# Layer 1's triangular inverses, taken pair by pair from k's projection on, in small steps between dense products

## The chip, the core and the metric

The kernel runs on one NeuronCore of one Trainium2 chip. The core has TensorE (PE in the profile; its weight loads are PEld), VectorE (DVE), ScalarE (ACT), GpSimd (POOL) and SyncE (SP), which here issues every transfer. Each takes its instructions in order and waits on semaphores. The metric is the device time of one execution in microseconds, as the median of several runs; lower is better.

## The reference, cut to what matters

One inference step through two layers, 1104 token columns in all (64 of samples, 16 meta tokens, 1024 of a prompt). Layer 0 is a gated DeltaNet and is not touched. Layer 1 is RWKV-7 time mixing:

```python
xs = xn[None] + xx[None] * mu[:, None, None, :]          # six token-shifted inputs
rkvz = jnp.einsum('sbtd,sde->sbte', xs[:4], w_rkvz)       # r, k, v, z: 1024 x 1024 each
w = -jax.nn.softplus(-(w0 + jnp.tanh(xs[4] @ w1) @ w2)) - 0.5
a = jax.nn.sigmoid(a0 + (xs[5] @ a1) @ a2)
kk = l2norm((k * k_k).reshape(B, T, H, N))
k = k * (1.0 + (a - 1.0) * k_a)
decay = jnp.exp(-jnp.exp(w))
b_h = kk * a_h
def step(S, inp):                                         # once per token
    r_t, k_t, v_t, d_t, kk_t, b_t = inp
    S = (S * d_t[:, :, None, :]
         + jnp.einsum('bhvk,bhk->bhv', S, -kk_t)[..., None] * b_t[:, :, None, :]
         + v_t[..., None] * k_t[:, :, None, :])
    return S, jnp.einsum('bhvk,bhk->bhv', S, r_t)
```

16 heads of width 64. The kernel takes the scan in chunks of 64 tokens: within a chunk each token's update depends on the earlier ones through a 64 x 64 unit lower triangle, made of products of the keys (kk, decayed) with kk * a, and the chunk needs that triangle's inverse. The triangles depend on k, on the decay w and on the rate a, but not on r, v or z.

## The kernel before

**Layout.** Channels lie on partitions and tokens along the free axis, in three segments of 384, 384 and 336 columns (SEGS, padded to 1152 in DRAM). A *pair* is one of 8 groups of 128 channels, two heads; an *item* is one pair in one segment: 6 chunks x 2 heads. There are 24 items. Dense products are taken in three terms (high and low parts of input and weight), so that one tile of 128 outputs by 1024 inputs costs 72 matmuls (24 for each segment). PSUM tiles carry a letter of their tag in front of their names in the profile: d for dense products, f for short-lived ones, m for the merges.

**Order.** Nothing is placed by hand. The program is written down in one order; a planner then fills each engine's queue: at each planned moment an engine takes, of what it could run by then (inputs there, a buffer free), the instruction that was written first. What is written early runs early if it can, and gives way otherwise. On the chip the queues are then fixed and in order. Buffers go around by tag: a tag with two buffers lets a third user wait. A pool that takes the place of closed ones gets its first tile when what overlaps it is through.

**The stages around the change.** At the end of layer 0, `gdn_out_norm` normalises the activations, with a pool "rnorm" on the right end of SBUF, directly under the xb tiles; `lora_first` (L1107) makes the hidden rows hh and hl of the two low-rank projections, and mixes k's inputs into slots. Then `layer1` (L1681):

1. `keys_decay_rate` (L1155), with a pool "lora": zero pads for five DRAM arrays, the second low-rank weights (w2: the matrices of w and of a), and then for each pair p: the 72 products of k's tile (`project`, L1145, stores it to kd), `lora_second` (L1135) for w with a sigmoid and a running sum (csd), and for a with a sigmoid (ad). Weights come by `load_w` (L189) through the tags wraw (2 buffers), whi and wlo (3 each).
2. A pool "rinv" for the inverses opens when "lora" is closed. A loop of 16 tiles, eight of r and then eight of v; before each eight, `mix` (L1011) makes eight inputs in eight of eleven slots, taken around in turn (a slot is two rows of xa or xc, or two tiles of xn2). After the tiles 1, 3, 5, 7 and 9 one call of `rwkv_inverse` (L1279) writes down a batch of five items, the last of four.
3. `rwkv_inverse`: for each item it loads csd, ad and kd (one item ahead), makes the keys (`rwkv_keys`, L1256: kk with a scale, Dp and iD with Exp; `alpha`, L1267, for al), 12 products of al with kk for the triangles (tile fL, stored to rltd) and one for the keys' row sums (frss, stored to rssd). Then, for the batch: `block_scale` (L487), and `inverse_blocks` (L455), which reloads the triangles' 32 x 32 diagonal blocks as rows, inverts them all at once on VectorE by 31 steps of two instructions (`inverse32`, L440), sends the result through DRAM into T1n and TT; and for each item `inverse_merge` (L504): 12 products (mY), a scaling on VectorE (invY), 12 more (mU), a copy, and a store to ttd.
4. `mix_out` stores two segments of z's input; `rwkv_gates` (L1027) makes z's first segment, 8 tiles of 24 products (tile dz), with its inputs in xa.
5. The pools close, and the recurrence begins: `rwkv_front` (L1323) reloads everything for an item, `rwkv_step` runs the chunks. Items there are numbered by segment and then pair, n = 8 s + p.

## Time and profile before

| what | us |
|---|---|
| median of 3 runs | 2517.23 (2510.52 to 2519.47) |
| the profiled execution | 2503.36 |
| its span, first to last instruction | 2501.6 |
| k's projection, from the last product of `lora_first` on | about 1396 to 1508 |
| r's eight tiles | about 1508 to 1640 |
| v's eight tiles | about 1640 to 1802 |
| z's first segment | about 1802 to 1866 |

In the views a time is in microseconds from the span's start. A row of a timeline gives start, length, engine, line, operation, out<-in, shapes, a count of instructions merged into the row, and in brackets how long the engine had been idle and what ended that. A row of a stretch gives for each engine its busy time and its number of instructions, then the granted clock of TensorE, the share of the DMA engines and GB/s. A row of waits gives who waited for whom: total us, times, longest. A row of groups gives count, busy time, mean length in ns, idle time before and what ended it. Matmuls are pipelined: a matmul of 384 columns has 0.34 us in a row, but the next one starts about 0.17 us after it, so PE's busy time tells whether it had work, and counts of matmuls tell how much it got done.

### The profile page before, as it was taken

How to read it: one execution, taken by the hardware profiler on the slowest of the kernel's cores; microseconds unless marked ns; L12 is line 12 of the kernel's file. 1: busy time of each engine (PE TensorE's matmuls, PEld its weight loads, DVE VectorE, ACT ScalarE, POOL GpSimd, SP SyncE). 2: the span in 40 equal slices, each digit the busy share in tenths (PEclk: the TensorE clock that was granted, in tenths of full speed). 3: DMA queues.
4: the chain of work that ended last, by engine and by line, in shares of the span. 5: the costliest groups of instructions: out<-in, count | busy, mean ns of one | idle time of the engine just before them, and what ended most of it. 6: DMA issues, size and time to landing. Idle time of an engine off the chain costs nothing. (4 is left out here: it accounts for less than half of the span.)

```text
span 2501.6 us, 52567 instructions
## 1 busy us (share of the span) xinstructions
PE 2305.2 (92%) x18593; PEld 2065.5 (83%) x18593; DVE 1698.5 (68%) x4268; ACT 1423.3 (57%) x3913; POOL 1148.4 (46%) x1404
## 2 busy tenths in 40 slices
PE   6998999999898989999989999988879999999996
PEld 5887988888797889789989998877768777877875
DVE  7779686876849585863357535697875678667563
ACT  5456555564646565565344557464444567678663
POOL 4554444444444354432214425453347565656653
PEclk9999999999999999999999999999988999999997
DMA  3323333333232333353251445767565444343331
GB/s 107 100 72 98 83 106 83 95 85 85 79 91 77 87 89 85 92 147 118 89 147 60 117 167 180 170 184 202 145 181 170 126 133 121 94 140 88 110 97 50
DMA packets 471939, 284.65 MB, mean 114 GB/s; under 512 B 187482, under 2 KB 457051, under 8 KB 471675
## 3 DMA queue, kind: packets, MB, share of 16 engines
q1 hardware_dynamic: 471674, 281.29, 40.0%
q8 instruction: 147, 2.41, 0.4%
q14 instruction: 118, 0.96, 0.1%
HBM read 200.00 MB, written 81.17 MB: 112 GB/s over the span
## 5 line engine op out<-in xcount | busy, mean ns | idle before, releaser
L86 POOL TENSOR_TENSOR wlo<-wraw,whi 128x512 fp32r<-128x512 f32 x260 | 347.8, 1340 | 350.9 <-ACT whi L82 311.9
L82 ACT CAST whi<-wraw 128x512 fp32r<-128x512 f32 x260 | 160.1, 617 | 168.7 <-PE dq L76 43.6
L76 PE MATMUL d<-xc,whi 128*128 128x384 f32 (+3 forms) x846 | 238.2, 339 | 0.3 <-ACT ev L1152 0.3
L450 DVE TENSOR_TENSOR invtmp<-invA,invT 72x31 f32<-72x31 f32 (+31 forms) x403 | 184.7, 458 | 20.8 <-DMA invA<-ltd 7.6
L452 DVE TENSOR_TENSOR invT<-invT,invtmp 72x31 f32<-72x31 f32 (+31 forms) x403 | 187.6, 466 | 6.9
L76 PEld LDWEIGHTS d<-xc,whi 128*128 128x128 f32 (+1 forms) x846 | 155.0, 190 | 7.3 <-issue 4.6
L76 PE MATMUL dz<-xc,whi 128*128 128x384 f32 (+1 forms) x480 | 149.6, 343 | 0.0
L76 PE MATMUL dv<-xc,whi 128*128 128x384 f32 (+1 forms) x480 | 149.4, 343 | 0.0
L417 DVE SCALAR_TENSOR_TENSOR cvy<-raw,cw,cvy 128x408 f32<-128x408 f32 (+2 forms) x192 | 128.9, 674 | 28.7 <-POOL cvy L415 27.4
L76 PE MATMUL dz<-xa,whi 128*128 128x384 f32 (+1 forms) x416 | 139.4, 357 | 4.8 <-ACT whi L82 2.4
L76 PE MATMUL d<-xa,whi 128*128 128x384 f32 (+3 forms) x450 | 140.0, 344 | 3.9 <-ACT xa L82 2.5
L415 POOL TENSOR_TENSOR cvy<-cvy,cvz 128x408 f32<-128x408 f32 (+2 forms) x96 | 99.7, 1039 | 70.5 <-ACT cvz L62 51.3
L76 PE MATMUL d<-xc,wlo 128*128 128x384 f32 (+2 forms) x396 | 130.5, 339 | 0.0
L76 PE MATMUL rA<-rS,AR 128*64 128x128 f32 x512 | 106.0, 289 | 8.7 <-DVE rS L1439 5.0
L76 PE MATMUL rA<-UV,G 128*64 128x64 f32 x1152 | 112.4, 223 | 0.4 <-ACT UV L62 0.4
L76 PE MATMUL dv<-xa,whi 128*128 128x384 f32 (+1 forms) x288 | 101.4, 352 | 8.9 <-ACT raw L401 6.9
L76 PEld LDWEIGHTS rA<-UV,G 128*64 128x64 f32 x1152 | 101.7, 138 | 3.3 <-issue 1.4
L62 ACT ACTIVATE o<-rA,gcol 128x128 f32<-128x128 f32 x128 | 46.2, 367 | 90.0 <-DVE S L774 89.6
L62 ACT ACTIVATE raw<-cvy 128x408 f32<-128x408 f32 (+2 forms) x96 | 49.5, 516 | 82.1 <-DVE cvy L417 80.6
L1439 DVE SCALAR_TENSOR_TENSOR rS<-rA,DC,pre 64x64 f32<-64x64 f32 x256 | 72.2, 282 | 31.6 <-PE rA L76 26.6
L62 ACT ACTIVATE rX<-rA,rk 64x64 f32<-64x64 f32 x272 | 83.7, 308 | 16.9 <-PE rA L76 10.9
L76 PE MATMUL dz<-xa,wlo 128*128 128x384 f32 (+1 forms) x256 | 90.5, 354 | 2.9 <-POOL wlo L86 2.9
(510 smaller groups left out, 7730.1 us busy)
## 6 DMA issues: line engine op xcount, KB each, us to landing
wraw<-in_gdn_w_in SPq DMA_DIRECT2D x96, 256.0 KB
wraw<-in_rwkv_w_rkvz SPq DMA_DIRECT2D x96, 256.0 KB
Sb<-in_state_gdn SPq DMA_DIRECT2D x64, 256.0 KB
wraw<-in_rwkv_w_o SPq DMA_DIRECT2D x48, 256.0 KB
E<-drow SPq DMA_DIRECT2D x24, 384.0 KB
attn<-drow SPq DMA_DIRECT2D x24, 384.0 KB
wraw<-in_gdn_w_out SPq DMA_DIRECT2D x36, 256.0 KB
out_s_gdn<-Sb SPq DMA_DIRECT2D x32, 256.0 KB
```

The costliest lines, as they stand in the source:

```text
L62: return self.nc.scalar.activation(out, in_, func, bias=bias, scale=scale, **kw)
L76: self.nc.tensor.matmul(out, lhsT, rhs, start=start, stop=stop)
L82: nc.scalar.copy(hi, x)
L86: e.tensor_tensor(lo, x, hi.bitcast(F32), op=ALU.subtract)
L415: nc.gpsimd.tensor_tensor(y[:, 0:wd], y[:, 0:wd], y1[:, 0:wd], op=ALU.add)
L417: nc.vector.scalar_tensor_tensor(y[:, 0:wd], raw[:, k:k + wd], cw[k], y[:, 0:wd], op0=ALU.mult, op1=ALU.add)
L450: nc.vector.tensor_tensor(tmp, A[:, j, j + 1:32].unsqueeze(2).broadcast_to([nb, n, m]), Tv[:, j, 0:m].unsqueeze(1).broadcast_to([nb, n, m] ...
L452: nc.vector.tensor_tensor(Tv[:, j + 1:32, 0:m], Tv[:, j + 1:32, 0:m], tmp, op=ALU.subtract)
L1439: nc.vector.scalar_tensor_tensor(S[hs[h], h, :], dS, DC[hs[h], ci:ci + 1], pre[hs[h], hs[h]], op0=ALU.mult, op1=ALU.add)
```

## The change

The inverses are started in k's projection. Items are numbered n = 3 p + s, so that a pair's three items follow one another, and the first can be made when the pair's k, w and a are there. `rwkv_inverse` becomes a generator that stops between small steps (48 in all): the keys of an item are made one step before its triangles' products, a batch's blocks are a step, and its merges come two to a step. At each stop it tells which pair must be projected before it goes on. After each of k's tiles two steps are taken, after each of r's and v's tiles three, and at the end what is left.

To have "rinv" open beside "lora", memory is rearranged: "lora" moves to the right end of SBUF; the raw w2 loses its tile and comes in four pieces through wraw, written down ahead of k's first weights; the zero pads shrink to one row that is broadcast; the loaded keys and the tiles T1n and L21 lie in xa; invA has one buffer, and Y and the row sums share a tile. Since xa's first four rows are taken by that, the mixed inputs go around in nine slots instead of eleven. The row-scale column and ttd's place follow the new numbering.

```diff
@@ inverse_blocks, inverse_merge
-        A = self.t(pool, [128, 1024], "invA", 2)[0:nb]
+        A = self.t(pool, [128, 1024], "invA", 1)[0:nb]
...
-        Y = self.t(pool, [128, 192], "invY", 2)[:, 0:32 * n].rearrange("p (c i) -> p c i", i=32)
+        Y = self.inv_yk[:, 192 * (th0 // 6 % 2):192 * (th0 // 6 % 2) + 32 * n].rearrange("p (c i) -> p c i", i=32)
@@ mix
-        xs = [self.slots[(self.slot + k) % 11] for k in range(8)]
+        xs = [self.slots[2 + (self.slot + k) % 9] for k in range(8)]
@@ keys_decay_rate
-        with self.tc.tile_pool(name="lora", bufs=1, reuse_waits="tile") as pool:
-            z = t(pool, [128, 8, 48], "zpad")
+        with self.tc.tile_pool(name="lora", bufs=1, side="right", reuse_waits="tile") as pool:
+            z = t(pool, [128, 48], "zpad")
...
-                nc.sync.dma_start(d[:, :, NT:1152].rearrange("k p n -> p k n"), z)
+                nc.sync.dma_start(d[:, :, NT:1152].rearrange("k p n -> p k n"), z.unsqueeze(1).broadcast_to([128, 8, 48]))
...
-            wr = t(pool, [128, 2, D], "lw2")
-            for q in (0, 64):
-                nc.sync.dma_start(wr[q:q + 64, 0], i["rwkv_w2"][0])
-                nc.sync.dma_start(wr[q:q + 64, 1], i["rwkv_a2"][0])
             w2 = t(pool, [128, 2, D], "lw2h", dt=F32R), t(pool, [128, 2, D], "lw2l", dt=F32R)
-            nc.scalar.copy(w2[0], wr)
-
-            for u, q in ((0, slice(0, 64)), (1, slice(64, 128))):
-                nc.vector.tensor_tensor(w2[1][q, u], wr[q, u], w2[0][q, u].bitcast(F32), op=ALU.subtract)
+            for u, (nm, q) in enumerate((("rwkv_w2", slice(0, 64)), ("rwkv_a2", slice(64, 128)))):
                 nc.gpsimd.memset(w2[1][64 - q.start:128 - q.start, u].bitcast(F32), 0.0)
+                for c in (0, 512):
+                    wr = t(self.wp, [128, 4, 128], "wraw", 2).rearrange("p k m -> p (k m)")
+                    for a in (0, 64):
+                        nc.sync.dma_start(wr[a:a + 64], i[nm][0][:, c:c + 512])
+                    nc.scalar.copy(w2[0][:, u, c:c + 512], wr)
+                    nc.vector.tensor_tensor(w2[1][q, u, c:c + 512], wr[q], w2[0][q, u, c:c + 512].bitcast(F32), op=ALU.subtract)
...
                 self.lora_second(1, k, hl, w2, dst_a)
+                self.inverse_go(2, k)
@@ the steps
+    def inverse_go(self, n, done):
+        while n and self.inv_need is not None and self.inv_need <= done:
+            self.inv_need = next(self.inv, None)
+            n -= 1
+
+    def inverse_load(self, n):
+        p, s = divmod(n, 3)
+        c0 = SEGS[s][0]
+        ld = dict(zip(("cs", "a", "k"), self.inv_ld[n % 2]))
+        for nm, d in (("cs", self.csd), ("a", self.ad), ("k", self.kd)):
+            self.nc.sync.dma_start(ld[nm], d[p][:, c0:c0 + 384])
+        return ld
+
+    def inverse_keys(self, n, pool):
+        nc, t = self.nc, self.t
+        p, s = divmod(n, 3)
+        ld = self.inverse_load(n)
+        kk, Dp, iD = self.rwkv_keys(p, ld, pool, "s")
+        sq = t(pool, [128, 384], "sgl", 2)
+        self.act(sq, kk, AF.Square)
+        al = t(pool, [128, 6, 64], "sal", 1)
+        self.alpha(al, kk, Dp, s, nc.vector)
+        nc.gpsimd.tensor_tensor(kk, kk, ld["a"], op=ALU.mult)
+        nc.vector.tensor_tensor(kk, kk, iD, op=ALU.mult)
+        return kk, al, sq
@@ rwkv_inverse
+        nxt = self.inverse_keys(items[0], pool)
         for q, n in enumerate(items):
-            s, p = divmod(n, 8)
...
-            ld = self.ahead or self.rwkv_load(n, pool, "s", names)
-            kk, Dp, iD = self.rwkv_keys(p, ld, pool, "s")
-
-            self.ahead = self.rwkv_load(n + 1, pool, "s", names) if n < 23 else None
...
+            yield min(n + 1, items[-1]) // 3
+            kk, al, sq = nxt
+            if n < items[-1]:
+                nxt = self.inverse_keys(n + 1, pool)
             gp = self.ps("f", 2, "L")
...
+        yield 0
         rk2 = self.rk2[:, 30 * b:30 * b + nth]
         blk = self.block_scale(ssd, rk2, pool)
         TT = [t(pool, [128, 6, 64], "sTT", 3) for _ in items]
-        T1n, L21 = t(pool, [128, 30, 32], "T1n", 1), t(pool, [128, 30, 32], "L21", 1)
+        T1n, L21 = self.inv_bl
         self.inverse_blocks(f"r{b}", ltd, blk, pool, TT, T1n[:, 0:nth], L21[:, 0:nth], nth)
         for q, n in enumerate(items):
+            if q % 2 == 0:
+                yield 0
             self.inverse_merge(L21, TT[q], T1n, rk2[:, 6 * q:6 * q + 6], pool, 6 * q, 6)
-            nc.sync.dma_start(self.ttd[n], TT[q].rearrange("p c k -> p (c k)"))
+            nc.sync.dma_start(self.ttd[8 * (n % 3) + n // 3], TT[q].rearrange("p c k -> p (c k)"))
+        yield min(items[-1] + 1, 23) // 3
@@ layer1
-        self.keys_decay_rate(x, self.hh, self.hl)
         ip = pool("rinv", ctx)
         self.rwkv_masks(ip, True)
+        self.inv_yk = self.t(ip, [128, 384], "invYK")
+        flat = xa.rearrange("p k n -> p (k n)").bitcast(F32)
+        self.inv_ld = [[flat[:, 384 * (3 * u + v):384 * (3 * u + v) + 384] for v in range(3)] for u in (0, 1)]
+        self.inv_bl = [flat[:, 2304 + 960 * u:3264 + 960 * u].rearrange("p (c i) -> p c i", i=32) for u in (0, 1)]
+        self.inv, self.inv_need = (p for b in range(5) for p in self.rwkv_inverse(b, ip)), 0
+        self.keys_decay_rate(x, self.hh, self.hl)
...
-            if n in (1, 3, 5, 7, 9):
-                self.rwkv_inverse((1, 3, 5, 7, 9).index(n), ip)
+            self.inverse_go(3, 7)
         self.mix_out(3, xb)
+        self.inverse_go(99, 7)
```

More of the change, by code (lines that the diff above doesn't have):

```diff
@@ L1275, in alpha @@
                                   kk[:, 0:64].rearrange("p (b r) -> p b r", r=8)[:, :, 0:1])
-    ahead = None
+    def inverse_go(self, n, done):
[21 more added lines that the diff above has]
+        return kk, al, sq
     def rwkv_inverse(self, b, pool):
@@ L1284, in rwkv_inverse @@
         ltd, ssd = self.dram([nth, 128, 64], f"rltd{b}"), self.dram([nth, 128], f"rssd{b}")
+        nxt = self.inverse_keys(items[0], pool)
         for q, n in enumerate(items):
-            s, p = divmod(n, 8)
-            names = ("cs", "a", "k")
-            ld = self.ahead or self.rwkv_load(n, pool, "s", names)
-            kk, Dp, iD = self.rwkv_keys(p, ld, pool, "s")
-            self.ahead = self.rwkv_load(n + 1, pool, "s", names) if n < 23 else None
-            sq = t(pool, [128, 384], "sgl", 2)
-            self.act(sq, kk, AF.Square)
-            al = t(pool, [128, 6, 64], "sal", 1)
-            self.alpha(al, kk, Dp, s, nc.vector)
-            nc.gpsimd.tensor_tensor(kk, kk, ld["a"], op=ALU.mult)
-            nc.vector.tensor_tensor(kk, kk, iD, op=ALU.mult)
+            yield min(n + 1, items[-1]) // 3
+            kk, al, sq = nxt
+            if n < items[-1]:
+                nxt = self.inverse_keys(n + 1, pool)
             gp = self.ps("f", 2, "L")
@@ L1306, in rwkv_inverse @@
             nc.scalar.copy(gl, gp[:, 0:384].rearrange("p (c i) -> p c i", i=64))
-            if s == 0:
+            if n % 3 == 0:
                 nc.gpsimd.tensor_tensor(gl[:, 0, :], gl[:, 0, :], self.m_strs2, op=ALU.mult)
             nc.sync.dma_start(ltd[6 * q:6 * q + 6].rearrange("c q i -> q c i"), gl)
-            kc = t(pool, [2, 384], "rkc", 1)
+            kc = self.inv_yk[0:2]
             nc.vector.tensor_copy(kc, ssp[0:2, 0:384])
             nc.sync.dma_start(ssd[6 * q:6 * q + 6].rearrange("c (h i) -> h c i", h=2), kc.rearrange("h (c i) -> h c i", c=6))
+        yield 0
         rk2 = self.rk2[:, 30 * b:30 * b + nth]
```

2 lines of the change are left out of this document (1 added, 1 removed).

## The prediction

> **What bounds the kernel now.** I read the page first, then busy time by stretch, then PE's waits, then single rows of the timeline.
>
> ```profile
> span 2501.6 us, 52567 instructions
> PE 2305.2 (92%) x18593; PEld 2065.5 (83%) x18593; DVE 1698.5 (68%) x4268; ACT 1423.3 (57%) x3913; POOL 1148.4 (46%) x1404
> ```
>
> TensorE (PE) is busy for 92% of the span and the other engines at most 68%, so only what takes time off PE's queue, or out of its gaps, counts. The change touches one part, layer 1 before its recurrence, about 1396 to 1866 us. Its stages by stretch (busy us and instructions for PE, PEld, DVE, ACT, POOL, then clock, DMA share, GB/s):
>
> ```profile
> 1396.00:1508.00 112.00, 110.36 (x648) 107.82 (x646) 40.38 (x51) 62.26 (x125) 33.40 (x40) 1.00 0.53 170
> 1440.00:1500.00 60.00, 60.00 (x361) 60.00 (x360) 19.40 (x26) 30.94 (x63) 16.01 (x17) 1.00 0.48 164
> 1508.00:1640.00 132.00, 126.31 (x1009) 112.11 (x1010) 85.90 (x171) 77.82 (x167) 61.53 (x98) 0.97 0.65 173
> 1640.00:1802.00 162.00, 143.27 (x1506) 121.88 (x1505) 133.64 (x305) 82.30 (x176) 62.03 (x92) 0.95 0.69 180
> 1802.00:1866.00 64.00, 51.94 (x601) 45.67 (x600) 49.69 (x99) 26.77 (x58) 29.57 (x33) 0.86 0.58 160
> ```
>
> The stretches are k's projection, a clean piece of it, r's, v's, and the gate product z. k's stage is full: 361 matmuls in 60 us are 0.166 us each, with no gap and the clock at 1.00. The others are not. How full they could be follows from what PE does in them: the same stretches for the dense products alone (tile d; r, v), for the triangles' products (fL; r, v), for the merges' second products (mU; r, v, z), where only engines with such instructions have columns, and PE's timeline rows of one pair's products.
>
> ```profile
> 1508.00:1640.00 132.00, 104.61 (x573) 98.53 (x574) 0.00 (x0) 10.52 (x24) 0.97 0.65 173
> 1640.00:1802.00 162.00, 107.94 (x565) 96.97 (x563) 0.00 (x0) 10.81 (x24) 0.95 0.69 180
> ```
>
> ```profile
> 1508.00:1640.00 132.00, 11.94 (x288) 9.78 (x288) 5.23 (x11) 0.97 0.65 173
> 1640.00:1802.00 162.00, 13.22 (x288) 11.26 (x288) 6.21 (x13) 0.95 0.69 180
> ```
>
> ```profile
> 1508.00:1640.00 132.00, 1.34 (x48) 1.04 (x48) 0.63 (x2) 0.97 0.65 173
> 1640.00:1802.00 162.00, 9.42 (x312) 7.09 (x312) 8.93 (x28) 0.95 0.69 180
> 1802.00:1866.00 64.00, 6.60 (x216) 5.17 (x216) 5.32 (x17) 0.86 0.58 160
> ```
>
> ```profile
> 1699.17 0.92 PE L76 MATMUL fL<-sal,skk 64*64 64x64 f32 x24 [1.37 <-DVE skk L1297]
> 1700.02 0.81 PE L76 MATMUL frss<-sgl,hmask 128*2 128x384 f32 x2
> ...
> 1706.51 0.56 PE L76 MATMUL mY<-T1n,L 32*32 32x32 f32 x22
> ```
>
> A pair costs PE 0.92 + 0.81 = 1.73 us to make its triangle and, with mY at 0.56 and mU about the same, 1.15 us to merge. fL and mU come 24 to a pair, so 12 triangles are made in r and 12 in v, and 2, 13 and 9 pairs merged in r, v and z. Then r needs 573 x 0.166 + 12 x 1.73 + 2 x 1.15 = 118 of its 132 us, v 565 x 0.166 + 12 x 1.73 + 13 x 1.15 = 130 of 162, z, with 8 tiles of 24 products, 192 x 0.166 + 9 x 1.15 = 42 of 64. PE loses 14 + 32 + 22 = 68 us. No change of order alone can gain more than these 68. Their causes, PE's waits in 1508 to 1866:
>
> ```profile
> PE fL L76 <- DVE skk L1297: 8.1, 7, 2.5
> PE fbpp L73 <- DMA invR<-rssd: 3.9, 3, 1.8
> PE dz L76 <- POOL wlo L86: 2.9, 4, 1.0
> PE mU L76 <- DVE invY L516: 2.9, 4, 1.6
> ```
>
> They are many and small: a triangle product that waits for VectorE, a load of row sums, the z weights.
>
> **The change, part by part.** The sum is made against the profiled execution, 2503.36 us (span 2501.6); the median of the runs shown, 2517.23, lies 13.9 above, so I add the difference to the median.
>
> *Work on PE.* Nothing is added or removed: 24 triangles, 24 merges, 5 block inversions, 24 projections. 16 of the 48 steps (10 triangles, 5 merges: 10 x 1.73 + 5 x 1.15 = 23 us) move into k's stage, which has no gap to take them: it grows by 23 us and later stages shrink by 23. Zero by itself.
>
> *The second LoRA weights (w2) go through "wraw".* Before, w2 has its own raw tile, and k's first weights are fetched long ahead. SyncE's (SP's) rows and the cast that ends the trip:
>
> ```profile
> 1338.86 0.39 SPq L197 DMA_DIRECT2D wraw<-in_rwkv_w_rkvz  x1
> ```
>
> ```profile
> 1341.43 0.62 ACT L82 CAST whi<-wraw 128x512 fp32r<-128x512 f32 x1 [1.30 <-DMA wraw<-in_rwkv_w_rkvz]
> ```
>
> One trip is 1341.43 - 1338.86 = 2.6 us. After, four pieces of w2 ask for the two wraw buffers ahead of k's weights. They are fetched at about 1339, but hold both buffers until they are copied into w2's tiles, and these now lie in a pool on the right, directly under xb, where by the code's sizes (22.7 KB a partition over 15.3 KB) they cover the normalisation pool, with its rsq tiles, and the last of layer 0's stored outputs. When these come free is seen here:
>
> ```profile
> 1396.04 0.42 POOL L1160 MEMSET zpad<- 128x384 f32 x1
> 1400.49 0.95 POOL L1133 TENSOR_TENSOR xa<-rsq,xa 64x336 fp32r<-64x336 f32 x1 [1.08 <-ACT xa L1132]
> ```
>
> zpad, first of the old pool, is written the moment the last LoRA product is through (1396.0); the last reader of rsq ends at 1400.49 + 0.95 = 1401.4. So two pieces are copied at about 1399 to 1402, two more take a trip of 2.6 us, k's weights another, plus two casts (0.62) and subtractions: k's first product comes 9 to 14 us after 1396. Besides, k's first tile is filler before:
>
> ```profile
> 1380.00:1396.00 16.00, 8.84 (x40) 8.56 (x41) 0.00 (x0) 0.00 (x0) 0.89 0.01 3
> ```
>
> ```profile
> 1379.80 0.42 PE L76 MATMUL dlora<-xh,xa 128*128 128x336 f32 x1 [2.33 <-ACT xh L82]
> 1380.90 0.52 PE L76 MATMUL d<-xc,wlo 128*128 128x384 f32 x1
> ```
>
> In 1380 to 1396 PE does 40 of its products (40 x 0.166 = 6.6 us) where the LoRA product waits for ScalarE. After, there is nothing to fill with. The rows also show what a gap costs behind it: 2.33 us idle, then a single product of 0.52 us, and a granted clock of 0.89 over these 16 us, some 2 us lost. Some 2 us of the LoRA second products (ready once two pieces are in) go into the gap. Sum: 11.5 + 6.6 + 2 - 2 = +18 us. Bounds: 0, if k's weights should keep their place, and 14 + 6.6 + 4 = 25.
>
> *Nine activation slots for eleven.* r's inputs had two slots free ahead; now none (the first is hh/hl, read until k's end). The one gap at r's start before:
>
> ```profile
> 1517.02 0.61 PE L76 MATMUL d<-xa,whi 128*128 128x336 f32 x1 [2.46 <-ACT xa L82]
> ```
>
> ```profile
> L62 ACT ACTIVATE mixs<-xb,omu 128x384 f32<-128x384 f32 (+3 forms) x34 | 17.1, 526 | 2.8 <-POOL xa L86 1.3 <-DVE xa L86 0.9 <-DVE xc L86 0.3
> ```
>
> 2.46 us there, with 6 pieces of 24 mixed ahead. Six more pieces behind k cost ScalarE 6 times 0.53 and a cast of at most the 0.62 quoted above, 6.9 us, partly under triangles: +5 at r, and +2 at v, where one slot is free instead of three: +7 (0 to 12).
>
> *ScalarE's function tables.* k's stage runs Sigmoid; the triangles' keys run Exp (sDp, siD). Before, the two never mix: one load at k's start, one at its end. The second, and the activation behind it:
>
> ```profile
> 1514.38 1.28 ACT L62 ACT_TABLE_LOAD   x1
> 1515.67 0.52 ACT L62 ACTIVATE sDp<-sldcs 128x384 f32<-128x384 f32 x1
> ```
>
> A load takes 1.28 us and the next activation starts 0.01 us later. After, each k tile has 6 sigmoids and some 2 to 3 Exps, placed as their inputs land: at least 2 loads a tile (16), at most two for every Exp of 10 pairs (40).
>
> ```profile
> L62 ACT ACTIVATE skk<-sldk,pcol 128x384 f32<-128x384 f32 x13 | 8.0, 616 | 0.0
> L62 ACT ACTIVATE siD<-sldcs 128x384 f32<-128x384 f32 x13 | 6.8, 525 | 13.0 <-DVE skk L1297 12.9
> L62 ACT ACTIVATE sDp<-sldcs 128x384 f32<-128x384 f32 x13 | 6.8, 519 | 6.4 <-issue 4.2 <-DVE sal L1271 2.2
> L62 ACT ACTIVATE sgl<-skk 128x384 f32<-128x384 f32 x12 | 6.2, 517 | 2.2 <-DMA rltd<-sgl 1.9 <-PE frss L76 0.3
> L1306 ACT COPY sgl<-fL 128x384 f32<-128x384 f32 x11 | 5.2, 475 | 13.4 <-issue 6.0 <-PE fL L76 3.7 <-POOL wlo L86 3.6
> ```
>
> ScalarE (ACT) is busy 62.3 us of k's 112; 10 pairs add 10 x (0.62 + 0.53 + 0.52 + 0.52 + 0.48) = 27, in a stage of 112 + 23 = 135: 89 us without loads, 110 with 16, 140 with 40. The keys also wait on ACT for loads that follow their own stores through DRAM, and the copies that free PE's product buffers are queued behind them. At the low end the loads hide under PE except where they stand ahead of the copy that frees a product's PSUM buffer; at the high end ACT is the bound and every load is PE's. I take a little over half a us for each of 16: +9 (0 to +30). The Trainium skill (ScalarE: Activation LUTs, "What ACT_TABLE_LOAD costs") gives 1.28 us and a drain, 2.66 in all, for a switch; the row agrees on the load and shows no drain. By the page's estimate 16 switches would be 43 us and ACT 132 of 135: the bound would nearly be reached.
>
> *z without merges.* 9 merges leave the stage (their PE time is counted above). Their transfers block SP:
>
> ```profile
> 1850.02 6.23 SPq L484 DMA_DIRECT2D sTT<-r_u  x12
> ```
>
> 12 issues hold the queue for 6.2 us with z's weights behind them. But the wait for wlo above is z's own: 192 products over 16 weight halves that pass through two wraw buffers. Of 22 us lost I keep 10: -12 (-20 to 0). The recurrence does not begin earlier than z's end:
>
> ```profile
> 1862.08 0.75 DVE L516 TENSOR_TENSOR invY<-mY,rk 32x192 f32<-32x192 f32 x2
> 1862.85 1.16 DVE L1233 TENSOR_SCALAR lnw<-pcol 128x8 f32<-128x8 f32 x1
> ```
>
> Its first tile (lnw) comes directly behind the last invY, though it needs a constant alone and VectorE was idle for 14 us of the stretch; its pool waits for the old ones to close, and "ev" stays in use until z ends.
>
> *The stalls in r and v.* 14 + 32 less the mixing gap (about 6) is 40 us. Pacing gives a third of the triangles a projection between keys and product, and the batch start (fbpp) too. But merges come at least a block inversion, several projections, after they are written down, so they still run the moment they are ready, as now; the waits on invY, and PE's in-order queue behind them, stay. -6 (-30 to +5).
>
> *SP.* 10 pairs bring 5 transfers each into k's stage, a batch some 30: at the 0.39 us of an issue quoted above 10 x 5 x 0.39 + 30 x 0.39 = 31 us, beside 11 issues a tile (8 x 11 x 0.39 = 34) in 135 us. It fits; what waits on SP for a store to land stands ahead of weights that are fetched a tile early.
>
> *Free:* the key, T1n and L21 tiles in xa, one invA, Y in a shared tile, the zero pads by broadcast. One invA puts a trip (2.6 us) more between batches, hidden as long as the inversions end before z; uncovered it would cost 4 trips, 10 us.
>
> Sum: 18 + 7 + 9 - 12 - 6 = +16 us, 2519 for the profiled execution, 2533 for the median.
>
> **The rivals.**
> 1. *The stalls go* (ends faster). If the chain of inversions is what paces PE from 1508 to 1866, starting it under k's projection frees r, v and z: -20 in z and -30 in r and v, against 18 + 5 + 2: -25, 2492. For it: v loses 32 us and z 22, with inversions in both. Against: PE waits for z's weights and keys too. It decides from 34 us gone (18 + 7 + 9), and shows from 47.
> 2. *ScalarE becomes the bound in k's stage.* 40 loads: 140 us of ACT in 135, before its waits; +30 instead of +9: 2533 + 21 = 2554. The Trainium skill (ScalarE: Activation LUTs, "Rules for kernel authors") says to group functions by table set; by that rule this rival is what comes. For it: keys come as their loads land, between sigmoids. Against: without loads ACT has 46 us free.
> 3. *Nothing moves:* w2's delay is small, since k's weights come first, and the stalls only move with the pairs: 7 + 9 - 12 - 6 = -2, 2515.
>
> **How the numbers follow.** Under 0.5% (12.6 us) a measurement of this kernel can hardly tell from none. Forecast 0.48 (2533; its own range 2512 to 2560), rival 1 0.24, rival 2 0.12, rival 3 0.16. The forecast lies over the bound with 0.42 and within with 0.06; rival 1 is faster with 0.22. Faster 0.23, same 0.23, slower 0.54. The range, 2486 to 2566, takes in most of rival 1 and rival 2.
>
> **What would show it.** Right: a gap of about 10 us on PE near 1396 with wraw's first rkvz transfer after 1400 instead of 1339; 16 to 40 table loads; more idle at r's start; no mU in z, and z in 45 to 52 us. Wrong: k's first product at 1396 as before; r and v with under 15 us of stalls; the recurrence's first tiles well before z's end.

## The result, and the profile after

The change makes the kernel slower: 2557.03 us median against 2513.88, a ratio of 1.0174 (95% interval 1.0150 to 1.0197), some 43 us. The forecast was 16 us slower with a range of 2486 to 2566: the sign and the range held, the size did not.

The page of the changed kernel begins so:

```profile
span 2556.5 us, 52563 instructions
PE 2323.6 (91%) x18593; PEld 2078.3 (81%) x18593; DVE 1691.2 (66%) x4270; ACT 1442.2 (56%) x3930; POOL 1144.8 (45%) x1404
```

PE's busy time grew by 18 us with the same 18,593 instructions, so it is not only idle for longer: some of its products take longer too. Of the 55 us between the two profiled executions 7 lie ahead of the change: the LoRA product that waits for xh (1379.80 us before, quoted in the prediction) comes here:

```profile
1386.67 0.42 PE L76 MATMUL dlora<-xh,xa 128*128 128x336 f32 x1 [2.32 <-ACT xh L82]
```

The rest lies before the recurrence. The stages of the changed kernel, cut at the ends of their last dense products (LoRA's end to k's, then r, v, z; columns as in the prediction's first table), and k's stretch again for the dense products, the second LoRA products, the triangles and the first merge products (tiles d, flora, fL, mY; the first two columns are PE and PEld). A triangle is, as in the prediction, the set of twelve of one item; the prediction calls an item a pair.

```profile
1401.30:1573.40 172.10, 137.67 (x843) 124.58 (x844) 72.53 (x136) 87.77 (x162) 48.20 (x80) 0.87 0.54 155
1573.40:1737.70 164.30, 145.43 (x1415) 125.39 (x1416) 117.13 (x241) 94.36 (x201) 64.94 (x99) 0.93 0.60 164
1737.70:1869.40 131.70, 123.39 (x1187) 112.69 (x1187) 96.19 (x214) 64.99 (x138) 51.09 (x63) 0.97 0.60 156
1869.40:1917.70 48.30, 43.07 (x362) 38.29 (x360) 14.87 (x28) 20.78 (x47) 24.04 (x22) 0.93 0.52 156
```

```profile
1401.30:1573.40 172.10, 112.35 (x576) 104.86 (x576) 0.00 (x0) 9.34 (x21) 0.87 0.54 155
```

```profile
1401.30:1573.40 172.10, 21.52 (x80) 14.09 (x80) 21.48 (x40) 0.87 0.54 155
```

```profile
1401.30:1573.40 172.10, 6.12 (x144) 5.28 (x144) 2.81 (x6) 0.87 0.54 155
```

```profile
1401.30:1573.40 172.10, 0.80 (x24) 0.58 (x24) 0.71 (x2) 0.87 0.54 155
```

Lost PE time is reckoned as in the prediction: the length, less 0.166 us for each dense or LoRA product, 1.73 for each triangle, 1.15 for each merge. k: 576 x 0.166 + 80 x 0.166 + 6 x 1.73 + 0.6 for one merge begun = 120 of 172 us, 52 lost. The kernel before, cut the same way (1396.0, 1502.1, 1634.2, 1801.9, 1858.8), loses 3. In the same manner for every kernel that was run (one profiled execution each, so a difference of a few us says little; the ratio to the kernel before is from all runs):

| kernel | ratio (95% interval) | lost in k | r | v | z |
|---|---|---|---|---|---|
| before | 1 | 3 | 14 | 34 | 18 |
| after | 1.0174 (1.0150-1.0197) | 52 | 31 | 17 | 12 |
| e1 k's weights first | 1.0092 (1.0076-1.0108) | 37 | 27 | 18 | 14 |
| e2 no steps in k | 1.0320 (1.0303-1.0337) | 29 | 15 | 35 | 66 |
| e3 Tanh | 1.0165 (1.0144-1.0186) | 47 | 30 | 20 | 16 |
| e4 stores from ScalarE | 1.0153 (1.0138-1.0168) | 48 | 35 | 17 | 13 |
| e5 before, nine slots | 1.0036 (1.0019-1.0053) | 3 | 19 | 30 | 25 |
| e8 before, one invA | 1.0069 (1.0047-1.0092) | 3 | 14 | 30 | 27 |
| e9 e1 + second invA | 1.0070 (1.0045-1.0095) | 39 | 29 | 15 | 7 |
| e10 e1 + other order | 1.0128 (1.0101-1.0156) | 35 | 34 | 20 | 10 |
| e12 e1 + e3 + e4 + e9 | 1.0049 (1.0026-1.0073) | 29 | 33 | 17 | 8 |
| e13 e1 + row sums in m | 1.0449 (1.0419-1.0479) | 36 | 32 | 16 | 107 |
| e14 e1, one step a tile | 1.0154 (1.0117-1.0190) | 13 | 38 | 24 | 38 |
| e15 e1, six steps in r, v | 1.0054 (1.0027-1.0081) | 37 | 33 | 14 | 7 |
| e16 e1, none in k, six | 1.0221 (1.0202-1.0240) | 7 | 22 | 32 | 56 |
| e17 e12, six steps in r, v | 1.0108 (1.0093-1.0123) | 27 | 43 | 16 | 7 |
| e18 e12, one step a tile | 1.0087 (1.0060-1.0114) | 12 | 35 | 24 | 21 |

Read across (after, e2, e3 and e4 hold the wait at k's start in k): the change takes 17 us off v's loss and 6 off z's, and adds 49 in k and 17 in r. The table stops at z's last dense product. From there to the end of the span the kernel before takes 643 us, after 639 and e8 656; every other kernel lies between 633 and 642. Three things can be seen in the trace of after.

*The start of k.* SP's queue, then ScalarE's casts, then PE:

```profile
1345.75 1.13 SPq L1174 DMA_DIRECT2D wraw<-in_rwkv_w  x2
1349.22 1.10 SPq L1174 DMA_DIRECT2D wraw<-in_rwkv_w  x2
...
1411.62 2.55 SPq L1174 DMA_DIRECT2D wraw<-in_rwkv_a  x4
1416.49 6.61 SPq L197 DMA_DIRECT2D wraw<-in_rwkv_w_rkvz  x4
```

```profile
1408.20 1.14 ACT L1175 CAST lw2h<-wraw 128x512 fp32r<-128x512 f32 x2 [2.60 <-POOL xa L1133]
```

```profile
1408.87 1.01 PE L76 MATMUL flora<-xa,lw2h 128*128 128x384 f32 x2 [7.53 <-ACT lw2h L1175]
...
1419.85 1.29 PE L76 MATMUL d<-xc,whi 128*128 128x384 f32 x3 [8.83 <-ACT whi L82]
```

The first two w2 pieces are fetched into both wraw buffers from 1346 to 1350 and are copied at 1408.2, once the pool for w2's tiles has come free. Only then do the last pieces and k's weights (1416.5) follow; k's first dense product starts at 1419.9, where the kernel before had done 40 of them by 1396. Between 1401.3 (LoRA's end) and 1419.9 PE does four products. The five stores of the zero pads, from a tile of the same pool, stand in SP's queue ahead of the last w2 pieces, from 1408.3 to 1411.5.

*The steps inside k.* PE's waits for ScalarE between 1420 and 1606 us (us in total, times, longest), ScalarE's longest wait, and ScalarE's table loads:

```profile
PE flora L76 <- ACT ev L62: 8.6, 7, 1.9
PE d L76 <- ACT ev L1152: 7.9, 3, 5.5
```

```profile
ACT ev L1152 <- DMA ad<-ev: 17.7, 8, 6.0
```

```profile
L62 ACT ACT_TABLE_LOAD x15 | 19.2, 1283 | 0.3
```

Before ScalarE can copy a dense product out of PSUM it waits 17.7 us, in 8 pieces, for one of three staging buffers (ev), which is still being stored. This wait by itself is not new. In the kernel before it is, from 1396 to 1502:

```profile
ACT ev L1152 <- DMA ad<-ev: 10.2, 8, 2.7
```

There the longest piece is 2.7 us, and PE waits for a copy of k's products for 0.3 us in all. The longest piece in after: SP's queue ahead of it, ScalarE's row, and two stretches of 10 us with the clock in the third column from the end:

```profile
1510.19 0.92 SPq L462 DMA_DIRECT2D xa<-rltd  x2
...
1517.13 1.39 SPq L197 DMA_DIRECT2D wraw<-in_rwkv_w_rkvz  x1
...
1521.17 1.62 SPq L1192 DMA_DIRECT2D ad<-ev  x2
```

```profile
1524.95 0.48 ACT L1152 COPY ev<-d 128x384 f32<-128x384 f32 x1 [5.99 <-DMA ad<-ev]
```

```profile
1520.00:1530.00 10.00, 4.52 (x14) 4.52 (x15) 7.12 (x20) 2.46 (x5) 0.14 (x1) 0.53 0.69 221
...
1590.00:1600.00 10.00, 6.63 (x19) 4.87 (x18) 5.36 (x8) 9.90 (x18) 0.92 (x4) 0.50 0.58 181
```

Between 1510 and 1520 SP issues the first batch's block transfers and the weights; the last stores of a go out at 1521.2, ScalarE gets its buffer at 1524.9, and PE stands for 5.5 us, until 1525.5. Behind that, PE runs at half speed: 14 products in 4.52 us are 0.32 us each, twice the 0.166 of a clean piece, at a granted clock of 0.53. From 1590 to 1600 there are several short waits, and the clock is 0.50. ScalarE (the fourth pair of columns) is busy for 9.90 of these 10 us, with three of the table loads among its work; so here, unlike in the stage as a whole (87.77 of 172.10 us), it is full.

*The chain of inversions.* It begins 74 us earlier (first triangle 1450.4 against 1524.5) but ends at 1882.7, 13 us after v's last dense product; before, it ended at 1865.7. So it takes 432 us instead of 341. One link, from one batch's copy out of invA to the next batch's first step, in after (ScalarE, SP, VectorE):

```profile
1665.95 2.06 ACT L470 COPY invA<-invT 120x1024 f32<-120x1024 f32 x1
```

```profile
1668.14 0.40 SPq L473 DMA_DIRECT2D r_u<-invA  x1
...
1673.65 7.13 SPq L484 DMA_DIRECT2D sTT<-r_u  x12
...
1685.01 1.90 SPq L467 DMA_DIRECT2D invA<-rltd  x2
```

```profile
1690.92 1.22 DVE L468 TENSOR_TENSOR invA<-invA,bblk 120x1024 f32<-120x1024 f32 x1 [2.92 <-DMA invA<-rltd]
```

and in the kernel before:

```profile
1739.30 1.77 SPq L467 DMA_DIRECT2D invA<-rltd  x2
```

```profile
1745.89 2.02 ACT L470 COPY invA<-invT 120x1024 f32<-120x1024 f32 x1 [4.92 <-DVE invT L452]
```

```profile
1746.18 1.93 DVE L468 TENSOR_TENSOR invA<-invA,bblk 120x1024 f32<-120x1024 f32 x1
```

Before, the next batch's blocks are loaded (1739.3) while the batch ahead is still being inverted, and VectorE goes on 0.3 us after the copy's start. After, invA is loaded at 1685.0, behind twelve transfers (7.13 us) and others that follow the store of its old content, and VectorE goes on 23 us after the copy has ended (1668.0). Among those others, at 1680.9, is the store of the last triangle of the batch that is to be loaded.

From the start of one copy to the next batch's first step the four links take 73, 25, 23 and 18 us in after; in the kernel before 11, -10, 0 and -4, where a minus means that the next batch started first. The longest has another cause than the shared tile: the first batch is copied out at 1556.5, but the second batch's last triangle is made at 1613.7 (no triangle begins between 1506.3 and 1553.7).

```profile
1613.72 0.91 PE L76 MATMUL fL<-sal,skk 64*64 64x64 f32 x24
```

```profile
1629.36 1.23 DVE L468 TENSOR_TENSOR invA<-invA,bblk 120x1024 f32<-120x1024 f32 x1 [4.12 <-DMA invA<-rltd]
```

### The profile page after: what moved, and what is told of

Read it like the earlier page. It is cut to its first block, busy times and chain, and to the rows that moved or that the text cites. A ratio compares the mean times of both kernels' runs of the same rounds, so it can differ in the third digit from the quotient of the medians.

```text
span 2556.5 us, 52563 instructions
## 1 busy us (share of the span) xinstructions
PE 2323.6 (91%) x18593; PEld 2078.3 (81%) x18593; DVE 1691.2 (66%) x4270; ACT 1442.2 (56%) x3930; POOL 1144.8 (45%) x1404
## 5 line engine op out<-in xcount | busy, mean ns | idle before, releaser
L76 PE MATMUL d<-xc,whi 128*128 128x384 f32 (+2 forms) x990 | 277.6, 344 | 19.5 <-ACT whi L82 8.8
L76 PEld LDWEIGHTS d<-xc,whi 128*128 128x128 f32 (+1 forms) x990 | 183.1, 193 | 29.7 <-ACT ev L1152 11.5
L76 PE MATMUL d<-xc,wlo 128*128 128x384 f32 (+3 forms) x468 | 155.3, 344 | 0.7 <-POOL wlo L86 0.7
L76 PEld LDWEIGHTS d<-xc,wlo 128*128 128x128 f32 (+1 forms) x468 | 89.7, 194 | 4.1 <-issue 2.0
L76 PEld LDWEIGHTS dz<-xc,whi 128*128 128x128 f32 x480 | 90.6, 194 | 0.7
```

The costliest lines, as they stand in the source:

```text
L76: self.nc.tensor.matmul(out, lhsT, rhs, start=start, stop=stop)
```

## The experiments

**e1, k's weights first.** The order in which the wraw buffers are asked for, alone:

```diff
+            early = [self.load_w(i["rwkv_w_rkvz"][0, 1][:, 128 * k:128 * k + 128]) for k in (0, 1)]
             w2 = t(pool, [128, 2, D], "lw2h", dt=F32R), ...
...
-                self.project(1, k, x, self.kd, k in (0,))
+                self.project(1, k, x, self.kd, k in (0,), early[k] if k < 2 else None)
```

> The kernel after, with the weights of k's first two tiles fetched ahead of the four w2 pieces. If the way of w2 through wraw is what delays k (first dense product of k at 1419.9 us after, 1380.1 before; 16 us of idle PE between 1401.0 and 1419.9), k's products fill the wait again and the kernel takes about 2535 us (2528 to 2542), 22 less than after. If the delay only moves, because the projection then waits for the LoRA products or for the pool all the same, it stays within 5 us of 2557.

2536.19 us, 21 less than after. k's products run again as filler between LoRA products, from 1390.85:

```profile
1390.85 0.34 PE L76 MATMUL d<-xc,whi 128*128 128x384 f32 x1
```

```profile
1432.30 1.01 PE L76 MATMUL d<-xc,whi 128*128 128x384 f32 x2 [5.54 <-ACT whi L82]
```

The last row shows what is left: the third tile's weights queue behind the w2 pieces now, 5.5 us. So the way of w2 through wraw is half of the loss.

**e2, no steps in k**, and **e14, one step a tile** (on top of e1): e2 takes the call behind each tile of k out, e14 puts 1 for 2.

```diff
-                self.inverse_go(2, k)
...
+                self.inverse_go(1, k)
```

> The kernel after without any inversion step inside k's projection: all 48 steps begin in r's. If the steps are what costs k's stage (186 us after against 112 before, of which 23 are work moved in), the stage falls back to about 115 us, r and v take the 23 us of work and some 10 to 15 us of stalls more, and the kernel takes about 2522 us (2512 to 2535). If starting early pays for itself in r, v and z, it takes 2550 or more.

> The kernel after with k's first weights ahead (ratio 1.009) and one step per tile of k instead of two, so that the merges of the first batch are written down behind k's last tiles. If k's and r's losses come with the steps written there (37 and 27 us of PE lost, against 3 and 14 before): half of the added 47 goes, and the chain, some 50 us later, puts less back: ratio about 1.003. If the end of the chain is what counts, it costs more than it saves: 1.012 or more.

e2 fell the other way: 2590.46 us, by the ratios 37 more than after. k's stage itself recovers, but z loses 66 us. e14: 1.0154, 16 us slower than e1; k loses 13 instead of 37, z 38 instead of 14. In z the merges stand in PE's queue between the dense products, and PE waits for the last batch's blocks. In e14 (the wait's end carries no semaphore event), and in e16, below, where it has one:

```profile
1863.68 1.24 PE L76 MATMUL mY<-xa 32*32 32x32 f32 x24 [18.82 <-issue]
```

```profile
1867.83 1.20 PE L76 MATMUL mY<-xa 32*32 32x32 f32 x24 [28.14 <-DMA xa<-r_t]
```

So in this kernel the early start is worth more than it costs; without it the chain sets the end of z. What the steps cost in k is real, as e2's first theory has it, but what they save in z is more.

**e3, Tanh for Sigmoid**, and **e4, two kinds of stores on ScalarE's queue** (in both one of two like edits is shown; e3 does the same for w, e4 for k):

```diff
-                self.act(f[:, 0:n], p[:, 0:n], AF.Sigmoid, bias=col["rwkv_a0"][:, k:k + 1])
+                self.act(f[:, 0:n], p[:, 0:n], AF.Tanh, scale=0.5, bias=hb[:, 8 + k:9 + k])
+                nc.vector.tensor_scalar(f[:, 0:n], f[:, 0:n], 0.5, 0.5, op0=ALU.mult, op1=ALU.add)
```

```diff
-                nc.sync.dma_start(self.ad[k][:, c0:c0 + n], f[:, 0:n])
+                nc.scalar.dma_start(self.ad[k][:, c0:c0 + n], f[:, 0:n])
```

> The kernel after with Sigmoid in k's stage as Tanh of half the argument, then times 0.5 plus 0.5 on VectorE (48 more VectorE instructions), so that ScalarE changes no table in that stage: 16 loads of 1.28 us fall away. By the prediction's term (a little over half a us of PE for each) 2548 us (2543 to 2552). If ScalarE is the bound of the stage, all 16 x 1.28 = 20 us and the waits behind them go: 2532 or less. If the stage is held by SyncE's queue and not by ScalarE: 2554 or more.

> The kernel after with the stores of k and of the rate a issued from ScalarE's queue, right behind the instruction that wrote them, instead of SyncE's. If k's stage is held because these stores stand in SyncE's queue behind the inversion's transfers and their waits (ScalarE waits 17.7 us for the landing of ad<-ev before it can copy a product out), the kernel takes about 2542 us (2535 to 2548). If issuing costs ScalarE as much as the wait, or the waits have another cause, 2553 to 2565.

2553.36 and 2549.89 us; by the ratios 2 and 5 us less than after, with intervals that overlap after's. e3 comes nearest to the third theory's time. No table load is left in k's stage, so the tables do not bound it: taking them out, net of 48 more VectorE instructions, brings 13 us at most by the ends of the intervals (1.0197 - 1.0144). In e4 ScalarE's wait for the stores of a is halved:

```profile
ACT ev L1152 <- DMA ad<-ev: 9.2, 7, 2.6
```

Against 17.7, 8 and 6.0 in after, and 10.2, 8 and 2.7 before. So the wait is shorter than in the kernel before, and yet k loses 48 us, 4 less than in after; the time lies between the two theories. Since the stores now cost ScalarE their issue, this is a net figure too. The order of the stores is at most one cause of several.

**e5 and e8, one part of the change in the kernel before.** Nine slots; one invA tile:

```diff
-        xs = [self.slots[(self.slot + k) % 11] for k in range(8)]
+        xs = [self.slots[2 + (self.slot + k) % 9] for k in range(8)]
```

```diff
-        A = self.t(pool, [128, 1024], "invA", 2)[0:nb]
+        A = self.t(pool, [128, 1024], "invA", 1)[0:nb]
```

> The kernel before with the inputs of r, v and z mixed into nine slots instead of eleven, and nothing else of the change. By the prediction's term +7 (0 to 12): about 2519 us against 2512 for before. If r's inputs are mixed in time all the same: 2510 to 2515.

> The kernel before with one invA tile instead of two, and nothing else of the change. The prediction put it at nothing, 10 us if uncovered: 2512 to 2522. If the shared tile is what stretches the chain of inversions (from the copy out of invA to the next batch's first step 17 to 24 us after, against 3 before), four batches end some 60 us later, most of it into the stage of z: 2540 to 2565.

e5: 1.0036, 9 us; by the table 5 more in r and 7 in z, 4 less in v. e8: 1.0069, 17 us, between the two theories. The link between batches becomes what it is in after:

```profile
1762.05 2.09 ACT L470 COPY invA<-invT 120x1024 f32<-120x1024 f32 x1 [1.09 <-DVE invT L452]
```

```profile
1774.26 2.84 SPq L467 DMA_DIRECT2D invA<-rltd  x2
```

```profile
1781.44 1.23 DVE L468 TENSOR_TENSOR invA<-invA,bblk 120x1024 f32<-120x1024 f32 x1 [6.32 <-DMA invA<-rltd]
```

19 us from the copy's start to the next batch, the last 6.32 of them VectorE waiting for the load. The chain then ends behind z: the last inversion is copied out at 1885, z's last dense product ends at 1868. So 13 of the 17 us lie where the table does not look (656 us from there to the end, against 643).

**e9, e10: what stretches the chain in after?** Both on top of e1. e9 gives the second and fourth batch a tile of their own in the room that the LoRA tiles leave; e10 writes a batch's triangles down in front of the merges of the batch ahead.

```diff
-        A = self.t(pool, [128, 1024], "invA", 1)[0:nb]
+        A = self.t(*((self.inv_p2, [128, 1024], "invA2", 1) if name in ("r1", "r3") else (pool, [128, 1024], "invA", 1)))[0:nb]
...
+        self.inv_p2 = ctx.enter_context(tc.tile_pool(name="rinv2", bufs=1, side="right", reuse_waits="tile"))
```

```diff
-    def rwkv_inverse(self, b, pool):
+    def rwkv_inverse(self, pool):
+        for b in range(6):
+            if b < 5:
+                yield from self.inverse_part(b, pool, 0)
+            if b:
+                yield from self.inverse_part(b - 1, pool, 2)
+            if b < 5:
+                yield 0
+                yield from self.inverse_part(b, pool, 1)
```

> The kernel after with k's first weights ahead (2536 us) and a second invA tile for the second and fourth batch, in the room that the LoRA tiles leave after k. If the shared invA holds the chain of inversions and the end of the chain holds z: about 2524 us (2515 to 2530). If neither PE's stalls nor z hang on the end of the chain: 2532 to 2540.

> The kernel after with k's first weights ahead (2536 us) and the steps in another written order: the triangles of a batch are written down behind the block inversion of the batch ahead and in front of its merges, instead of behind the merges. If writing the batches one whole batch behind the other is what stops the triangles (none between 1507 and 1554 us after, while VectorE inverts): the chain ends some 40 us earlier, no merges are left in z, and the kernel takes about 2520 us (2510 to 2528). If the pause comes from loads and queues and not from the written order: 2532 to 2540.

e9: 1.0070 against e1's 1.0092, as the first theory has it in size, but the intervals overlap; z's loss falls from 14 to 7. The third batch still starts 23 us after the second one's copy, although its tile is free and its last triangle is made by 1646, because the store of that triangle (1657.75) and the load stand in SP's queue behind the second batch's twelve transfers:

```profile
1644.77 0.92 PE L76 MATMUL fL<-sal,skk 64*64 64x64 f32 x24
```

```profile
1644.02 2.04 ACT L470 COPY invA<-invT 120x1024 f32<-120x1024 f32 x1
```

```profile
1651.74 5.91 SPq L484 DMA_DIRECT2D sTT<-r_u  x12
1657.75 0.39 SPq L1331 DMA_DIRECT2D rltd<-sgl  x1
...
1662.76 1.58 SPq L467 DMA_DIRECT2D invA<-rltd  x2
```

```profile
1669.08 1.23 DVE L468 TENSOR_TENSOR invA<-invA,bblk 120x1024 f32<-120x1024 f32 x1 [3.57 <-DMA invA<-rltd]
```

So in after the shared tile is not the only thing that holds the link: the order of SP's queue does so by itself. e10: 1.0128, not faster. The pause behind the first batch is gone, so it came from the written order: the first link takes 25 us instead of 71 in e1. But another pause of 42 us stands behind the second batch (no triangle from 1556 to 1598 us), and the inversions themselves, from first step to copy, take 238 us together instead of 199, so the chain ends where it did in e1; z loses 10 instead of 14, r 34 instead of 27.

**e13, row sums in another PSUM tag** (on top of e1).

```diff
-            ssp = self.ps("f", 2, "rss")
+            ssp = self.ps("m", 2, "rss")
```

> The kernel after with k's first weights ahead (ratio 1.009), and the row sums of a triangle in a PSUM buffer of the merges' tag (m) instead of the tag f, whose two buffers the LoRA products need in k's stage too. If the shared buffers make the waits of the LoRA products (PE waits 7.3 us for sigmoids of LoRA products between 1407 and 1600) and of the products behind them: ratio about 1.005 (1.003 to 1.007). If not: 1.008 to 1.011.

1.0449, 90 us slower than e1, and neither theory foresaw it. The triangles' row sums and the merges now pass through the same two buffers, the batches run one behind the other, and z waits for two of them:

```profile
1871.63 0.28 PE L76 MATMUL mY<-xa 32*32 32x32 f32 x2 [32.06 <-DMA xa<-r_t]
```

```profile
1937.58 1.18 PE L76 MATMUL mY<-xa 32*32 32x32 f32 x24 [38.14 <-DMA xa<-r_t]
```

k's loss (36 against 37) did not move: row sums in the tag f are not what costs k. The triangles' products and the LoRA products still share that tag.

**e15, e16, e17: the written pace.** Six steps behind each tile of r and v for three; e15 on e1, e16 on e1 without steps in k, e17 on e12.

```diff
-            self.inverse_go(3, 7)
+            self.inverse_go(6, 7)
```

> The kernel after with k's first weights ahead (ratio 1.009) and six steps written behind each tile of r and v instead of three. If the written pace sets the chain of inversions (ten steps a batch at three a tile of some 19 us are 63 us, and the batches of after stand 61 to 69 us apart in r and v), the chain ends some 40 us earlier, no merges are left in z, and the ratio is about 1.005 (1.003 to 1.007). If transfers and the shared invA set it: 1.008 to 1.011.

> The kernel after with k's first weights ahead, no steps in k's projection, and six steps behind each tile of r and v. At three a tile it would stand at 1.032 - 0.009 = 1.023. If the written pace makes the chain late there: about 1.009 (1.004 to 1.014), which is what the nine slots and the single invA cost by themselves, and the early start is then worth about nothing. If the early start itself is what counts: 1.020 or more.

> The four edits together (ratio 1.005) with six steps behind each tile of r and v. If the written pace counts: 1.001 (0.998 to 1.003). If not: 1.004 to 1.007.

e15: 1.0054, in the range of the first theory, but its interval touches e1's, and the chain does not end 40 us earlier (the last inversion is copied out at 1839 us, 427 after LoRA's end; in e1 at 1840, 434 after it). e16: 1.0221 where 1.023 was reckoned for three steps (that kernel was not run): no effect. e17: 1.0108, outside both theories, and worse than e12 by 15 us; the chain ends ahead of z, and r loses 43. No run shows the pace to be what makes the chain long. e16 against e15 gives the price of starting late: 42 us at this pace, 37 at the other (e2 against after).

**e12 and e18: the four edits together,** with two steps behind a tile of k and with one.

> Four edits together on the kernel after: k's first weights ahead, a second invA after k, the stores of k and a on ScalarE's queue, Tanh for Sigmoid. Singly they gave 21, some 5, 7 and 4 us. If they cost PE separate waits, the sum holds: 2557 - 37 = 2520, a ratio to before of about 1.003 (1.000 to 1.006). If ScalarE's order is the one bound behind the last three, freeing it in three ways opens more than the sum: below 0.998. If they cover for one another: 1.007 or more.

> The four edits together (ratio 1.005) with one step per tile of k instead of two. With a single invA half the steps cut k's loss from 37 to 13 us, but the chain then ended in z and cost 38 us there. If it was the shared invA that made the chain too long for the later start, the second one takes z's loss back to some 10 to 15 us and the kernel beats both: 0.995 (0.991 to 0.999). If the chain is too late even so: 1.003 or more.

e12: 1.0049, as the first theory has it; 31 us of the 43 are undone, about what e1, e3, e4 and e9 give singly by their ratios (21 + 2 + 5 + 5). PE's two longest waits that are left in k show what else stands in ScalarE's queue. ScalarE's row and PE's, twice:

```profile
1420.13 0.53 ACT L62 ACTIVATE sDp<-xa 128x384 f32<-128x384 f32 x1 [3.04 <-DMA xa<-csd]
```

```profile
1421.58 0.65 PE L76 MATMUL flora<-xa,lw2h 128*128 128x336 f32 x1 [3.49 <-ACT ev L62]
```

```profile
1469.67 0.61 ACT L62 ACTIVATE skk<-xa,pcol 128x384 f32<-128x384 f32 x1 [2.88 <-DVE skk L1308]
```

```profile
1471.56 1.01 PE L76 MATMUL d<-xc,whi 128*128 128x384 f32 x2 [3.91 <-ACT ev L1152]
```

The first time an instruction of the inversion's keys waits for a load (csd), and the activation that PE needs stands behind it. The second time three stores of a, which e4's edit put into this queue (1466.4 to 1469.6), then two instructions of the keys and the copy of a triangle stand ahead of the copy that PE needs. No run takes the keys out of this order, so its price is not known.

e18: 1.0087, as the second theory has it; z's loss is 21 instead of the 38 of e14, as the second invA was meant to do (two more edits lie between the two kernels), but still too high. No version beat the kernel before.

## Why the prediction was right and wrong

*w2 through wraw* (+18, 0 to 25): right, in size and in mechanism. e1 measures 21. The first rkvz transfer came at 1416.5 (forecast: after 1400), and k's first product 24 us after 1396 (forecast 9 to 14): LoRA itself ended 5 us later, the pool came free 7 us after that (1408.2; forecast 3 to 6), and five zero pads, put at nothing, two more pieces and a set of weights followed.

*Nine slots* (+7, 0 to 12): right in size; e5 measures 9. In mechanism it is right for r alone (5 by the table, as forecast). In v, where 2 were forecast, e5 loses 4 less, and the 7 in z were not forecast, so the total fits in part by luck.

*Function tables* (+9, 0 to 30): the count was right at its low end (16 loads from 1435.8 to 1607.3), the price was not borne out: 2 us by e3, not told from nothing. The quoted row of 1.28 us with no drain behind it carried; rival 2, ScalarE as the bound through 40 loads, is refuted for the stage by the count and by e3. By the drain that the Trainium skill adds in ScalarE: Activation LUTs, "What ACT_TABLE_LOAD costs" (2.66 us a switch), 16 switches are an estimated 43 us of ScalarE. The trace does not agree: the 15 rows of the stage add up to 19.2 us, with 0.3 us idle ahead of them, and the run without them is 2 us faster.

*z without merges* (-12): the stage took 48.3 us, inside the 45 to 52 forecast, but not for that reason: four merges still ran in it (96 mU, 72 mY). By the table z's loss fell by 6, not 12.

*The stalls in r and v* (-6): v's loss fell by 17, r's rose by 17, so nothing came of it.

*Work on PE, "zero by itself", and SP, "it fits"*: this is the step that failed. It held that 23 us of work move into k's stage and lengthen it by 23 us. The only price for waits in that stage was the 9 us of the tables. By e1, where the start of k is mended, k still loses 37 us where it lost 3, though only 6 triangles were made by its last product in after, instead of the 10 and 5 merges forecast. That the steps cost this is shown: k loses 7 us without them (e16), 13 with one a tile (e14) and 37 with two (e1). The moved work brings waits to a PE that had next to none: ScalarE, which takes its instructions in order, stands still for a staging buffer whose store is behind the inversion's transfers in SP's queue, or for the input of a key, and what PE needs stands behind. PE's longest waits also come with stretches at half speed. The sum of SP's issue times (31 + 34 us) fitted: 66 us by the trace. What was not costed is the order within the queues, and the clock. How the loss divides among these stays open: e3, e4 and e9 together bring 37 down to 29 (e12), the stores' order alone 52 to 48 (e4), and the row sums' PSUM tag has no part that shows (e13).

*One invA, "free"* (2.6 us a batch, 10 us uncovered): mis-sized. In the kernel before it costs 17 us (e8), where all four links take 18 to 20 us. On e1 a second tile gives back 5, not told apart from nothing (e9), since SP's order holds the link there too. Of what lengthens the chain to 432 us, the largest piece is the 73 us of the first link, which the written order makes; but with that order changed the other pieces grow (e10). The shared tile has a part, the written pace is not shown to have one (e15).

The early start is worth 37 to 42 us against the same kernel without it (e2, e16), but that kernel loses 56 to 66 us in z, where the one before loses 18. Against the kernel before, the early steps cost k and r more than v and z give back (e9, with the start of k mended and a second tile: k 39, r 29, v 15, z 7, together 90; before 69, and 8 of the difference are the nine slots by e5's row), and the change also gives up w2's own raw tile and two slots, 21 and 9 us.

Put together from e1 and e5, 30 of the 43 us are w2 and the slots, for which the prediction had 25. Everything else it had at +9 - 12 - 6 = -9, and it is about +13. The parts do not simply add up: one invA alone costs 17 in the kernel before. Rival 1 (the stalls go) needed 34 us of stalls gone; v and z gave 17 + 6. Rival 3 (nothing moves) is refuted by e1.

## What to carry to other kernels

A stage that runs PE without a gap has no room for more work just because other engines are idle for half of it: cost the order in the queues that the new work shares (SP's stores behind waiting loads, ScalarE's copies behind waiting stores and the new work's own instructions), not only the sum of the issue times. When an early start is paid for with buffers, cost both against the same chain: a start 74 us earlier ended 13 us inside the stage that it was meant to clear. And look at what asks for a ring buffer first: four small loads ahead of the weights cost more than any other part that could be measured by itself.

## What was unexpected of the hardware

The clock made the waits dearer than their length. After PE's wait of 5.5 us up to 1525.5 the granted clock is 0.53 in 1520 to 1530 and a product takes 0.32 us instead of 0.166, until 1530.8. In 1590 to 1600 no single wait is longer than 1.3 us, PE is busy for 6.6 of 10 us, and the clock is 0.50. Nor does it take a long wait: behind one of 1.85 us, up to 1568.1, there are 3.4 us at half clock (PE alone, then the clock):

```profile
1568.40:1571.70 3.30, 3.30 (x13) 0.50 0.25 40
```

In k's stretch PE was busy for 137.7 us with 120 us of work by the clean prices. Of these 18 us 12 lie in four stretches at half clock, of 20, 10, 10 and 3 us from 1404.5, 1493.3, 1520.6 and 1568.4 on, where PE is busy for 24 us with 12 of work: slow products, not idle time. The other 6 are not told apart.

The Trainium skill (TensorE: Matmul & The Clock Gate, Part 1: The HAM clock gate) has the clock halved after an idle window of about 3.4 us and back at full after as long a busy one. The wait of 5.5 us is longer than that, and half clock goes with it. But half clock is on record from 1520.6, 0.6 us into the wait, and full clock is back only 5.3 us after its end, so the lengths do not show here; and the wait of 1.85 us does not agree. For short waits that follow one another the same page (A second HAM failure mode: psum-queue depth-cycling) tells of another kernel whose clock swings between half and full. That agrees here: half from 1568.4, full (1.00) from 1571.8, half again (0.50) from 1582.1 to 1602.5.
